# Moving the transposes of attention weights by one slot in a two-layer hybrid decoder, with one PSUM ring, a held coefficient generator and a gate read from PSUM

## Chip, cores, metric

The kernel runs on one core of a Trainium2 chip. The metric is the device time of one execution in microseconds; the median of three executions is given.

## What is computed

Two layers, each with three token mixers in parallel over 512 tokens of width 1024: retention (A), stick-breaking attention (B) and a complex-diagonal state-space model (C). The change lies in mixer B and in what runs around it. Cut to that, the reference is

```python
def stick_breaking(q, k, v, q_norm, k_norm):          # 8 heads of 64, 512 tokens
    q, k, scale = rmsnorm(q, q_norm), rmsnorm(k, k_norm), SB_HEAD_DIM ** -0.5
    for blk in range(S_ // SB_BLOCK):                 # 4 blocks of 128 queries
        start, end = blk * SB_BLOCK, blk * SB_BLOCK + SB_BLOCK
        z = jnp.einsum('bqhd,bkhd->bhqk', q[:, start:end], k[:, :end]) * scale
        causal = jnp.arange(end)[None, :] < (start + jnp.arange(SB_BLOCK))[:, None]
        log_keep = jnp.where(causal, jax.nn.log_sigmoid(-z), 0.0)
        after = lax.cumsum(log_keep, axis=3, reverse=True) - log_keep
        w = jnp.where(causal, jnp.exp(jax.nn.log_sigmoid(z) + after), 0.0)
        outs.append(jnp.einsum('bhqk,bkhd->bqhd', w, v[:, :end]))
    return jnp.concatenate(outs, axis=1)
...
y_b = stick_breaking(...) * jax.nn.silu(sz)           # the gate
merged = sigmoid(ga) * (y_a @ proj_a) + sigmoid(gb) * (y_b @ proj_b) + sigmoid(gc) * (y_c @ proj_c)
x = x + merged @ w_out
```

## The kernel before

**Main pieces and slots.** All large products (the input projection, the three output projections, w_out) run as float32 split into a high and a low part, three matmuls each (`three`). They are cut into main pieces, most of 24 matmuls into one PSUM tile `mm`; a piece of `pb`, the projection of the gated attention output, has 12. `layer` runs through the list `mains`; one turn of that loop is a slot, and `now[0]` is its number. Everything else is written as generators which `spawn` puts into a slot. What a generator issues before `yield 0` goes to the engines ahead of the slot's main piece, what follows goes behind it, and `yield n` passes to n slots later. So the order on every engine is fixed by this loop when the program is built. Behind the main piece and the generators, `W.fill` splits the next weights, and then `background`, the generator of the state-space coefficients (`Coef`, mostly on GpSimd), is advanced until the shares counted in `load` are used up, unless the slot is in `quiet`.

**An attention pair.** `sb_pair(pr)` does two heads, h = 0 and 1; four pairs start 4 slots apart. With s the first slot of a pair:

- s: the preamble, which splits queries and keys into `qd`, `ql` and `ks` (ScalarE, VectorE, GpSimd).
- s+1 and s+3: scores of the last query block of head 0 and of head 1 into PSUM tile `z3` (3 matmuls); s+2 and s+4: the scores of the other three blocks into `z02` and `z1` (9 matmuls). Behind the main piece `weights_of` makes weights from them: two sigmoids on ScalarE, then on VectorE a reverse scan (`kp`, line 1083) and a product into `w3`, `w02` or `w1`.
- `turn(h)`: 10 transposes on TensorE (line 1100) of the weights of head h into three PSUM tiles `wt`; `turned(h)` copies them to SBUF (ScalarE two, VectorE one, line 1107). `turn(0)` stands in s+3 behind the z3 scores of head 1; `turn(1)` in s+5, where the next pair's z3 scores of head 0 (its own s+1) stand ahead of it.
- s+6: 16 matmuls with the values `sv` into PSUM tile `sbo`, behind the next pair's z02 and z1 scores; VectorE copies it to SBUF (line 1143). s+7: VectorE multiplies it by the gate `zb` (a silu made at slots 12 to 17 of the layer). s+8 (last pair: s+7): the result is split for `pb`.

Slots of a layer, by what the main piece is: 0 to 11 queries, keys and values of attention; 12 to 23 gates; 24 to 27 `cu` (the input of mixer C); 28 to 30 `cz`; from 31 on `pb`. The pairs start at slots 11, 15, 19 and 23.

**PSUM.** The eight banks are two rings: `ps_mm` has 3 for main pieces, `ps_sm` has 5 for everything else. A tile takes the bank of the allocation 3, or 5, earlier in its ring, so its first matmul waits until that one has been read.

**Coefficients.** `Coef.emit` makes four quarters. Per quarter it makes `ab` and `ct` (products on GpSimd), transposes them, makes `ca` and `b`, and multiplies these on TensorE (`pk`); the blocks are copied into `mt` (GpSimd). `quiet` holds slots 10 to 13 and 23 to 28 of the layer.

```python
        quiet = {*range(first - 1, first + 3), *range(turn, turn + 6)}
        for name, m in mains:
            ...
            for gen in due.pop(i, []):
                advance(gen, late)
            m()
            while late:
                advance(late.pop(0), late)
            W.fill()
            while i not in quiet and load["G"] < G_SHARE * load["T"] and load["V"] < V_SHARE * load["T"]:
```

Of the kernel before, what the change touches and what calls it, by code (L numbers as in the profile page):

```python
# [10 lines left out]
F32 = mybir.dt.float32  # L11
# [3 lines left out]
ALU = mybir.AluOpType  # L15
PSUM = bass.MemoryType.PSUM

P = 128
# [17 lines left out]
K = dict(  # L36

    nw=12, w=4, raw=4, b=48,

    sb0=0, sb_gap=4, ssm0=6, ssm_gap=3, ret0=9, ret_gap=3, x0=-3, x1=2, ret_pre=4, lead=15,  # L40

    g=0.9, v=0.7,

    n1=1, n2=1, q1=1, q2=1, k1=1, k2=2, s1=1, s2=1, s3=1, s4=2, s5=1, s6=1, s7=2, b1=1, b2=1, b3=1,
# [142 lines left out]
def trunk(ctx: ExitStack, tc, x_in, w_in, par_in, bc_in, ng_in, cst_in, rope_in, out):  # L187
    nc = tc.nc
# [12 lines left out]
    TT = counted(nc.vector.tensor_tensor, "V", 1.04e-3)  # L201
# [8 lines left out]
    bp = ctx.enter_context(tc.tile_pool(name="bp", bufs=B_BUFS))  # L210
    sp = ctx.enter_context(tc.tile_pool(name="sp", bufs=8))
    dp = ctx.enter_context(tc.tile_pool(name="dp", bufs=1, space=bass.MemoryType.DRAM))
    ps_mm = ctx.enter_context(tc.tile_pool(name="ps_mm", bufs=3, space=PSUM))
    ps_sm = ctx.enter_context(tc.tile_pool(name="ps_sm", bufs=5, space=PSUM))

    def bt(name, dt=F32, shape=(P, 512)):
        return bp.tile(list(shape), dt, tag="b", name=name)
# [2 lines left out]
        return sp.tile([P, n], F32, tag="s", name=name, padded_shape=[P, 64])  # L220

    def pmm():
        return ps_mm.tile([P, 512], F32, tag="mm", name="mm")

    def psm(name):
        return ps_sm.tile([P, 512], F32, tag="sm", name=name)


    cst = const.tile([P, NCST], F32, name="cst")
# [11 lines left out]
    def C(n):  # L241
# [9 lines left out]
        out=negm, in_=negm, pattern=[[1, P]], base=0, channel_multiplier=-1, compare_op=ALU.is_ge, fill=0.0  # L251
# [6 lines left out]
    now = [0]  # L258
# [38 lines left out]
    class Weights:  # L297
        def __init__(self):
            self.loaded = self.made = self.taken = self.free = 0
            self.raw, self.units = [], []  # L300
# [384 lines left out]
    class Coef:  # L685


        def __init__(self, l):
            self.l = l
            self.q = [None] * 4  # L690
            self.gen = self.emit()
            self.ready = -1
            self.used = 0
            self.start = 0

        def step(self):
            next(self.gen, None)
# [25 lines left out]
        def quarter(self, q, bb, cc):  # L723
# [14 lines left out]
            def v48(ap):  # L738
                return ap.rearrange("p (g j m) -> p g j m", g=4, j=8)

            while self.used < q - 1 or now[0] < self.start + K["ssm_gap"] * q:
                yield

            ab = [bt("ab0"), bt("ab1")]
# [35 lines left out]
            for i in range(2):  # L780
                h = slice(64 * i, 64 * i + 64)
# [12 lines left out]
            for i in range(2):  # L794
                h = slice(64 * i, 64 * i + 64)
# [45 lines left out]
    def layer(l, last, base):  # L841
# [3 lines left out]
        coef = coefs[l]  # L845
# [153 lines left out]
        zc, zb = [None] * 4, [None] * 4  # L999
# [47 lines left out]
        sbo = [None] * 4  # L1047

        def sb_pair(pr):
# [18 lines left out]
            def scores(ps, off, h, b):  # L1068
                n = 128 * (b + 1)
                c = slice(b * P, b * P + P)  # L1070
                MM(ps[:, off : off + n], qd[h][:, c], ks[h][:, 0:n], start=True, stop=False)
                MM(ps[:, off : off + n], ql[h][:, c], ks[h][:, 0:n], start=False, stop=False)
                MM(ps[:, off + n - P : off + n], identb, negm, start=False, stop=True)
# [19 lines left out]
            def turn(h):  # L1093
                pts = []
                for blocks in (
                    [(b, 0) for b in range(4)], [(1, 1), (2, 1), (3, 1), (3, 3)], [(2, 2), (3, 2)],
                ):
                    pt = psm("wt")
                    for i, (b, kb) in enumerate(blocks):
                        nc.tensor.transpose(pt[:, i * P : i * P + P], wblk(h, b, kb), ident)  # L1100
                    pts.append(pt)
                return pts

            def turned(h, pts):
                wt0[h], wt13[h] = bt("wt0"), bt("wt13")
                ACT(wt0[h], pts[0], AF.Copy)
                nc.vector.tensor_copy(out=wt13[h], in_=pts[1])
                ACT(wt2[:, 256 * h : 256 * h + 256], pts[2][:, 0:256], AF.Copy)

            for h in range(2):  # L1110
                ps = psm("z3")
                scores(ps, 0, h, 3)
                if h == 1:
                    pts = turn(0)
                yield 0
                w3[h] = bt("w3")
                weights_of(ps, [(0, 512)], w3[h])
                if h == 1:
                    turned(0, pts)
                yield K["b2"]  # L1120
                ps, ps1 = psm("z02"), psm("z1")
                scores(ps, 0, h, 0)
                scores(ps, 128, h, 2)
                scores(ps1, 0, h, 1)
                yield 0
                w02[h] = bt("w02")
                weights_of(ps, [(0, 128), (128, 384)], w02[h])
                weights_of(ps1, [(0, 256)], w1[:, 256 * h : 256 * h + 256])
                yield K["b3"]
            pts = turn(1)  # L1130
            yield 0
            turned(1, pts)
# [1 line left out]
            po = psm("sbo")  # L1134
# [5 lines left out]
                    MM(po[half[h], 128 * kb : 512], sv[kb][:, c], w, start=kb == 0, stop=kb == 3)  # L1140
            yield 0
            sbo[pr] = bt("sbo")
            nc.vector.tensor_copy(out=sbo[pr], in_=po)
            yield K["b5"]
            while zb[pr] is None:
                yield 1
            TT(out=sbo[pr], in0=sbo[pr], in1=zb[pr], op=ALU.mult)
            if pr < 3:
                yield 1
            yb[pr] = split(sbo[pr], "yb")  # L1150


# [220 lines left out]

        first = at["sv"] + 3 + K["sb0"]
        turn = first + 3 * K["sb_gap"]
        quiet = {*range(first - 1, first + 3), *range(turn, turn + 6)}
        for name, m in mains:
            i = now[0]
            quarters()
# [51 lines left out]
```

## Time and profile before

| | us |
|---|---|
| median of 3 executions | 1289.89 |
| lowest, highest | 1289.74, 1291.02 |
| profiled execution | 1291.43 |
| span of its records | 1289.7 |
| TensorE busy | 1271.6 |

The profiled execution took 1.73 us more than the span of its records, and 1.54 us more than the median. Its mean granted TensorE clock is 0.996 of full speed, which is 2.4 GHz. Durations below are from this execution. In rows, a line such as L197 is often that of a helper which records every matmul or tensor operation, so groups are told apart by their tiles, written output<-inputs. A matmul's row gives its start and the time until its modelled end; neighbours overlap, so the time of a group is best read from its start to the start of the next.

### The profile page before, as it was taken

The numbers are of one execution on the slowest core, as the hardware profiler recorded it, in microseconds if no ns is written. First come the engines' busy times: TensorE is split into PE (matmuls) and PEld (weight loads), VectorE is DVE, ScalarE is ACT, GpSimd is POOL, SyncE is SP. The second block draws the span as 40 slices with busy tenths as digits, with TensorE's granted clock in tenths as the row PEclk, the third lists the DMA queues.
The fourth block names the chain that finished last, engine by engine and source line by source line (L and its number), as shares of the span: only waits on it lengthen the run. The fifth ranks groups of instructions, "written<-read, shape, count | busy, mean of one in ns | idle before, by whom it ended". The sixth has DMA issues, their size and how long they took to land.

```text
span 1289.7 us, 16710 instructions
## 1 busy us (share of the span) xinstructions
PE 1271.6 (99%) x6388; PEld 1051.8 (82%) x6388; DVE 845.1 (66%) x1192; ACT 536.9 (42%) x919; POOL 388.4 (30%) x453
## 2 busy tenths in 40 slices
PE   8999999999999999999999989999999999999998
PEld 6887788888888888888888877888888888888887
DVE  6988976866784448555374678778657834675542
ACT  5444454454444433332343545534534544433311
POOL 3314743546531012000052136444565311210000
PEclk9999999999999999999999989999999999999999
DMA  5323222124223322234442312122231232222342
GB/s 211 101 96 98 67 66 82 66 82 131 66 66 99 98 75 72 84 97 155 147 166 72 98 49 66 49 83 82 96 101 66 70 127 82 66 82 83 97 137 75
DMA packets 37235, 119.53 MB, mean 93 GB/s; under 512 B 4130, under 2 KB 4770, under 8 KB 37156
## 3 DMA queue, kind: packets, MB, share of 16 engines
q1 hardware_dynamic: 29376, 104.87, 25.1%
q10 hardware_dynamic: 7780, 13.60, 3.1%
q8 instruction: 50, 0.82, 0.3%
q14 instruction: 29, 0.24, 0.1%
HBM read 114.26 MB, written 4.19 MB: 92 GB/s over the span
## 4 chain that ended last, share of the span: by engine, by line
PE 82%; DVE 3%; ACT 1%; issue 0%; DVEq 0%; ACTq 0%
PE mm L197 71%; PE T L411 2%; PE ro L197 2%; PE py L197 1%; DVE kp L1083 1%; PE S L197 1%; PE sbo L197 1%; PE wt L1100 1%; DVE w L197 1%; PE z L197 1%; PE rkv L197 1%; PE rs L197 1%; PE yaT L1269 1%; DVE ks L197 0%; DVE ybl L197 0%; PE pk L197 0%
## 5 line engine op out<-in xcount | busy, mean ns | idle before, releaser
L197 DVE TENSOR_TENSOR wl<-raw,wh 128x1024 fp32r<-128x1024 f32 x196 | 249.6, 1280 | 100.8 <-ACT wh L320 97.1
L197 PE MATMUL mm<-hh,wh 128*128 128x512 f32 x640 | 256.2, 400 | 0.0
L197 PE MATMUL mm<-hh,wl 128*128 128x512 f32 x640 | 250.8, 392 | 0.0
L197 PE MATMUL mm<-hl,wh 128*128 128x512 f32 x640 | 250.8, 392 | 0.0
L320 ACT ACTIVATE wh<-raw 128x1024 fp32r<-128x1024 f32 x196 | 206.3, 1058 | 61.8 <-PE mm L197 24.7
L197 PE MATMUL mm<-wh,hh 128*128 128x512 f32 x512 | 206.7, 404 | 0.4 <-ACT hh L434 0.4
L197 PE MATMUL mm<-wl,hh 128*128 128x512 f32 x512 | 201.8, 394 | 0.3 <-DVE wl L197 0.3
L197 PE MATMUL mm<-wh,hl 128*128 128x512 f32 x512 | 201.7, 394 | 0.0
L197 PEld LDWEIGHTS mm<-hh,wh 128*128 128x128 f32 x640 | 121.2, 189 | 25.6 <-issue 1.8
L197 PEld LDWEIGHTS mm<-hh,wl 128*128 128x128 f32 x640 | 120.7, 189 | 26.1
L197 PEld LDWEIGHTS mm<-hl,wh 128*128 128x128 f32 x640 | 121.0, 189 | 23.5
L197 PEld LDWEIGHTS mm<-wl,hh 128*128 128x128 f32 x512 | 104.8, 205 | 18.6 <-DVE wl L197 2.0
L197 PEld LDWEIGHTS mm<-wh,hl 128*128 128x128 f32 x512 | 104.5, 204 | 18.2 <-DVE hl L197 0.3
L197 PEld LDWEIGHTS mm<-wh,hh 128*128 128x128 f32 x512 | 104.6, 204 | 17.9 <-ACT hh L434 0.8
L1026 ACT ACTIVATE gate<-mm 128x512 f32<-128x512 f32 x48 | 28.6, 596 | 118.2 <-PE mm L197 118.2
L1083 DVE TENSOR_TENSOR_SCAN kp<-kp,zero 128x511 f32<-128x511 f32 (+1 forms) x64 | 60.3, 962 | 22.8 <-ACT kp L1079 22.7
L197 POOL TENSOR_SCALAR ms<-ss 128x8 f32<-128x8 f32 (+3 forms) x56 | 19.1, 341 | 181.9 <-DVE ss L855 101.0
L197 POOL TENSOR_TENSOR rs<-ms,mhalf 128x8 f32<-128x8 f32 (+3 forms) x56 | 64.7, 1155 | 4.7
L853 ACT ACTIVATE sq<-mm 128x512 f32<-128x512 f32 x32 | 19.0, 592 | 85.8 <-PE mm L197 85.7
L197 PE MATMUL mm<-wl,mgh 128*128 128x512 f32 (+1 forms) x136 | 51.5, 378 | 0.2
L197 PE MATMUL mm<-wh,mgh 128*128 128x512 f32 (+1 forms) x136 | 51.3, 377 | 0.0
L197 PE MATMUL mm<-wh,mgl 128*128 128x512 f32 (+1 forms) x136 | 51.3, 377 | 0.0
(258 smaller groups left out, 2244.5 us busy)
## 6 DMA issues: line engine op xcount, KB each, us to landing
raw<-in_w SPq DMA_DIRECT2D x196, 512.0 KB, 3.6
x<-in_x SPq DMA_DIRECT2D x8, 256.0 KB, 7.1
rope<-in_rope ACTq DMA_DIRECT2D x8, 256.0 KB, 4.1
xh<-in_x ACTq DMA_DIRECT2D x8, 256.0 KB, 4.8
x<-xh ACTq DMA_DIRECT2D x8, 256.0 KB, 2.0
xh<-x ACTq DMA_DIRECT2D x8, 256.0 KB, 4.5
out<-xh ACTq DMA_DIRECT2D x7, 256.0 KB, 2.0
br<-in_bc ACTq DMA_DIRECT2D x2, 256.0 KB, 2.9
```

Of the source, the lines that this page charges most:

```text
L197: return f(*a, **k)
L320: ACT(wh, raw, AF.Copy)
L411: nc.tensor.transpose(pt[:, i * P : i * P + P], src[:, i * P : i * P + P], ident)
L853: ACT(s2, ps, AF.Square)
L1026: ACT(sg, ps, AF.Sigmoid)
L1083: nc.vector.tensor_tensor_scan(v, v, zero1.to_broadcast([P, n - 1]), 1.0, ALU.mult, ALU.add)
L1100: nc.tensor.transpose(pt[:, i * P : i * P + P], wblk(h, b, kb), ident)
L1269: nc.tensor.transpose(pt[:, t * P : t * P + P], ytok[t][m // 4][:, (m % 4) * P : (m % 4) * P + P], ident)
```

## The change

It makes four edits.

1. In `sb_pair`, `turn(0)` moves from s+3 (behind the z3 scores of head 1) to s+4 (behind the z02 and z1 scores of head 1), and its copies go behind the weights of that slot. `yield K["b3"] + h` puts `turn(1)` from s+5 to s+6, which is the next pair's s+2; there it stands ahead of that pair's z02 and z1 scores. The `sbo` matmuls move from s+6 to s+7, ahead of the next pair's z3 scores of head 1.
2. The `sbo` copy to SBUF goes; the gate product takes `po` from PSUM, behind the main piece of s+7. The test for `zb` goes with it. The split is at s+8, for the last pair at s+7.
3. The PSUM rings of 3 and 5 become one ring of 8, in which every tile takes the bank of the eighth allocation before it.
4. `quiet` loses slots 23 to 28; instead every quarter of the coefficients but the first is held until slot `coef.hold` = turn + 5, which is 28.

```diff
--- before.py
+++ after.py
@@ -210,8 +210,7 @@
     bp = ctx.enter_context(tc.tile_pool(name="bp", bufs=B_BUFS))
     sp = ctx.enter_context(tc.tile_pool(name="sp", bufs=8))
     dp = ctx.enter_context(tc.tile_pool(name="dp", bufs=1, space=bass.MemoryType.DRAM))
-    ps_mm = ctx.enter_context(tc.tile_pool(name="ps_mm", bufs=3, space=PSUM))
-    ps_sm = ctx.enter_context(tc.tile_pool(name="ps_sm", bufs=5, space=PSUM))
+    ps = ctx.enter_context(tc.tile_pool(name="ps", bufs=8, space=PSUM))
 
     def bt(name, dt=F32, shape=(P, 512)):
         return bp.tile(list(shape), dt, tag="b", name=name)
@@ -220,10 +219,10 @@
         return sp.tile([P, n], F32, tag="s", name=name, padded_shape=[P, 64])
 
     def pmm():
-        return ps_mm.tile([P, 512], F32, tag="mm", name="mm")
+        return ps.tile([P, 512], F32, tag="ps", name="mm")
 
     def psm(name):
-        return ps_sm.tile([P, 512], F32, tag="sm", name=name)
+        return ps.tile([P, 512], F32, tag="ps", name=name)
 
 
     cst = const.tile([P, NCST], F32, name="cst")
@@ -691,7 +690,7 @@
             self.gen = self.emit()
             self.ready = -1
             self.used = 0
-            self.start = 0
+            self.start = self.hold = 0
 
         def step(self):
             next(self.gen, None)
@@ -738,7 +737,7 @@
             def v48(ap):
                 return ap.rearrange("p (g j m) -> p g j m", g=4, j=8)
 
-            while self.used < q - 1 or now[0] < self.start + K["ssm_gap"] * q:
+            while self.used < q - 1 or now[0] < (self.hold if q else 0) or now[0] < self.start + K["ssm_gap"] * q:
                 yield
 
             ab = [bt("ab0"), bt("ab1")]
@@ -1110,23 +1109,23 @@
             for h in range(2):
                 ps = psm("z3")
                 scores(ps, 0, h, 3)
-                if h == 1:
-                    pts = turn(0)
                 yield 0
                 w3[h] = bt("w3")
                 weights_of(ps, [(0, 512)], w3[h])
-                if h == 1:
-                    turned(0, pts)
                 yield K["b2"]
                 ps, ps1 = psm("z02"), psm("z1")
                 scores(ps, 0, h, 0)
                 scores(ps, 128, h, 2)
                 scores(ps1, 0, h, 1)
+                if h == 1:
+                    pts = turn(0)
                 yield 0
                 w02[h] = bt("w02")
                 weights_of(ps, [(0, 128), (128, 384)], w02[h])
                 weights_of(ps1, [(0, 256)], w1[:, 256 * h : 256 * h + 256])
-                yield K["b3"]
+                if h == 1:
+                    turned(0, pts)
+                yield K["b3"] + h
             pts = turn(1)
             yield 0
             turned(1, pts)
@@ -1140,13 +1139,9 @@
                     MM(po[half[h], 128 * kb : 512], sv[kb][:, c], w, start=kb == 0, stop=kb == 3)
             yield 0
             sbo[pr] = bt("sbo")
-            nc.vector.tensor_copy(out=sbo[pr], in_=po)
-            yield K["b5"]
-            while zb[pr] is None:
-                yield 1
-            TT(out=sbo[pr], in0=sbo[pr], in1=zb[pr], op=ALU.mult)
+            TT(out=sbo[pr], in0=po, in1=zb[pr], op=ALU.mult)
             if pr < 3:
-                yield 1
+                yield K["b5"]
             yb[pr] = split(sbo[pr], "yb")
 
 
@@ -1373,7 +1368,8 @@
 
         first = at["sv"] + 3 + K["sb0"]
         turn = first + 3 * K["sb_gap"]
-        quiet = {*range(first - 1, first + 3), *range(turn, turn + 6)}
+        quiet = range(first - 1, first + 3)
+        coef.hold = turn + 5
         for name, m in mains:
             i = now[0]
             quarters()
```

**Places.** TensorE, layer 1, around `turn(1)` of pair 0; `z3`, `z02` and `z1` are scores of pair 1, `mm` is a main piece, `sbo` the output of pair 0. Before, then after:

```order
L197 MATMUL z3_1243<-negm_80,identb_79 128x128
L1100 MATMUL wt_1247<-ident_78,w02_1221 128x128
L1100 MATMUL wt_1247<-ident_78,w1_997 128x128
L1100 MATMUL wt_1247<-ident_78,w02_1221 128x128
...
L1100 MATMUL wt_1257<-ident_78,w3_1136 128x128
L197 MATMUL mm_1260<-hh_82,wh_1085 128x512
...
L197 MATMUL z02_1323<-ks0_1169,qd0_1167 128x128
...
L197 MATMUL z1_1324<-negm_80,identb_79 128x128
L197 MATMUL sbo_1334<-wt0_1142,sv_836 64x512
...
L197 MATMUL mm_1343<-hh_82,wh_1147 128x512
```

```order
L197 MATMUL z3_1240<-negm_77,identb_76 128x128
L197 MATMUL mm_1244<-hh_79,wh_1082 128x512
...
L1099 MATMUL wt_1302<-ident_75,w02_1213 128x128
L1099 MATMUL wt_1302<-ident_75,w1_994 128x128
L1099 MATMUL wt_1302<-ident_75,w02_1213 128x128
...
L1099 MATMUL wt_1312<-ident_75,w3_1120 128x128
L197 MATMUL z02_1315<-ks0_1148,qd0_1146 128x128
...
L197 MATMUL z1_1316<-negm_77,identb_76 128x128
L197 MATMUL mm_1326<-hh_79,wh_1126 128x512
...
L197 MATMUL sbo_1379<-wt0_1225,sv_833 64x512
...
L197 MATMUL z3_1388<-ks1_1149,qd1_1147 128x512
```

The transposes stood directly behind the z3 scores and ahead of that slot's main piece; now a main piece of 24 matmuls stands between, and they are ahead of the z02 scores. `sbo` now has another main piece ahead of it.

VectorE, the same place: the copy `wt13` is part of `turned(1)`, `w02` and `w1` are weights of pair 1's head 0, `w3` of its head 1, `wl` is a weight split, `silu` a gate. Before, then after:

```order
L1083 SCALAR_TENSOR_TENSOR kp_1369<-kp_1369,zero1_85 128x383
L197 TENSOR_TENSOR w02_1368<-w02_1368,kp_1369 128x511
L1083 SCALAR_TENSOR_TENSOR kp_1375<-kp_1375,zero1_85 128x255
L197 TENSOR_TENSOR w1_1241<-w1_1241,kp_1375 128x255
L1143 COPY sbo_1380<-sbo_1334 128x512
L197 TENSOR_TENSOR wl_1383<-raw_1089,wh_1382 128x1024
L197 TENSOR_TENSOR sbo_1380<-sbo_1380,silu_1091 128x512
L197 TENSOR_TENSOR silu_1391<-mm_1343,silu_1391 128x512
L1083 SCALAR_TENSOR_TENSOR kp_1438<-kp_1438,zero1_85 128x511
L197 TENSOR_TENSOR w3_1437<-w3_1437,kp_1438 128x511
L1107 COPY wt13_1444<-wt_1402 128x512
```

```order
L1106 COPY wt13_1352<-wt_1307 128x512
L1082 SCALAR_TENSOR_TENSOR kp_1357<-kp_1357,zero1_82 128x127
L1082 SCALAR_TENSOR_TENSOR kp_1357<-kp_1357,zero1_82 128x383
L197 TENSOR_TENSOR w02_1356<-w02_1356,kp_1357 128x511
L1082 SCALAR_TENSOR_TENSOR kp_1363<-kp_1363,zero1_82 128x255
L197 TENSOR_TENSOR w1_1238<-w1_1238,kp_1363 128x255
L197 TENSOR_TENSOR wl_1369<-raw_1086,wh_1368 128x1024
L197 TENSOR_TENSOR silu_1377<-mm_1326,silu_1377 128x512
L197 TENSOR_TENSOR sbo_1418<-sbo_1379,silu_1088 128x512
L1082 SCALAR_TENSOR_TENSOR kp_1421<-kp_1421,zero1_82 128x511
L197 TENSOR_TENSOR w3_1420<-w3_1420,kp_1421 128x511
```

The `sbo` copy between `w1` and the weight split is gone, the product with the gate reads the PSUM tile (`sbo_1379`) a slot later, and `wt13` stands ahead of the scans of `w02` where before it stood behind `w3`.

GpSimd, layer 1: `ql` and `qd` are the preamble of pair 3, `mt` copies belong to quarter 0, `ab` and `ct` are quarter 1 of the coefficients. Before, then after:

```order
L197 TENSOR_TENSOR ab0_1779<-bbr_1311,y_re_213 128x512
L197 TENSOR_TENSOR ct_1781<-bbi_1312,y_im_214 128x512
L197 TENSOR_TENSOR ab0_1779<-ab0_1779,ct_1781 128x512
L197 TENSOR_TENSOR ab1_1780<-bbr_1311,y_re_213 128x512
L1062 MEMSET ql0_1793 64x512
L1065 COPY qd0_1789<-qd0_1789 64x512
...
L832 COPY mt0_1775<-kk_1868 32x256 x2
...
L832 COPY mt0_1775<-kk_1868 32x2x32 x2
L197 TENSOR_TENSOR ct_1785<-bbi_1312,y_im_214 128x512
L197 TENSOR_TENSOR ab1_1780<-ab1_1780,ct_1785 128x512
```

```order
L1061 MEMSET ql0_1762 64x512
L1064 COPY qd0_1758<-qd0_1758 64x512
...
L831 COPY mt0_1752<-kk_1855 32x256 x2
...
L831 COPY mt0_1752<-kk_1855 32x2x32 x2
L197 TENSOR_TENSOR ab0_2178<-bbr_1290,y_re_210 128x512
L197 TENSOR_TENSOR ct_2180<-bbi_1291,y_im_211 128x512
L197 TENSOR_TENSOR ab0_2178<-ab0_2178,ct_2180 128x512
L197 TENSOR_TENSOR ab1_2179<-bbr_1290,y_re_210 128x512
L197 TENSOR_TENSOR ct_2184<-bbi_1291,y_im_211 128x512
L197 TENSOR_TENSOR ab1_2179<-ab1_2179,ct_2184 128x512
```

Four products of quarter 1 (two on `ab0`, one on `ct`, one on `ab1`) stood ahead of the preamble and of the `mt` copies and now stand behind them; the other two of the six follow as before. Farther on, the `pk` matmuls of quarter 1 stand one `pb` piece of 12 matmuls earlier on TensorE, in both layers. Every engine but VectorE, which has the eight copies fewer, issues the same number of instructions of each kind.

## Rows read from the trace of the kernel before

**Rows 1.** The page, busy time by engine: us (share of the span) xinstructions.

```profile
PE 1271.6 (99%) x6388; PEld 1051.8 (82%) x6388; DVE 845.1 (66%) x1192; ACT 536.9 (42%) x919; POOL 388.4 (30%) x453
```

**Rows 2.** Waits of TensorE, whole span: line waited for, us in total, times, longest.

```profile
PE wt L1100 <- DVE w L197: 10.4, 10, 2.1
PE gain L452 <- POOL negm L249: 2.3, 1, 2.3
```

**Rows 3.** Windows: length, busy us (count) by engine, TensorE's granted clock, DMA, GB/s.

```profile
98.06:99.14 1.08, 1.08 (x12) 1.08 (x12) 0.71 (x2) 1.08 (x3) 0.00 (x0) 1.00 0.81 182
99.14:104.70 5.56, 5.56 (x27) 4.60 (x26) 5.35 (x11) 1.98 (x4) 0.00 (x0) 1.00 0.28 85
111.79:114.12 2.33, 1.48 (x12) 1.18 (x12) 2.23 (x4) 1.72 (x4) 0.00 (x0) 1.00 0.62 214
142.97:147.57 4.60, 2.35 (x12) 2.06 (x12) 4.39 (x6) 1.97 (x4) 0.58 (x1) 0.77 0.33 114
147.57:153.72 6.15, 6.15 (x26) 5.08 (x25) 6.05 (x6) 1.33 (x2) 6.07 (x4) 0.90 0.18 54
178.60:180.68 2.08, 1.30 (x12) 1.11 (x12) 1.91 (x5) 2.08 (x4) 0.00 (x0) 1.00 0.68 217
210.21:211.57 1.36, 1.23 (x12) 0.96 (x10) 1.36 (x2) 1.16 (x3) 0.00 (x0) 1.00 0.03 12
746.52:752.33 5.81, 2.36 (x13) 2.07 (x12) 5.60 (x7) 1.95 (x4) 4.82 (x3) 0.77 0.32 90
752.33:759.82 7.49, 7.49 (x26) 5.99 (x25) 3.67 (x4) 1.33 (x2) 0.68 (x2) 0.73 0.23 70
783.06:786.72 3.66, 1.48 (x12) 1.19 (x12) 3.45 (x5) 1.78 (x4) 0.16 (x1) 1.00 0.42 143
817.16:819.72 2.56, 1.52 (x13) 1.20 (x12) 2.38 (x6) 2.56 (x5) 0.00 (x0) 1.00 0.64 202
849.25:850.60 1.35, 1.22 (x11) 0.96 (x10) 1.35 (x2) 1.16 (x3) 0.00 (x0) 1.00 0.01 3
```

**Rows 4.** Timeline, TensorE: start us, us, line, out<-in, count [idle <-releaser].

```profile
98.12 1.26 PE L1100 MATMUL wt<-ident,w 128*128 128x128 f32 x10
...
759.82 0.22 PE L197 MATMUL z<-ks,qd 128*128 128x128 f32 x1
...
761.00 1.40 PE L197 MATMUL sbo<-wt,sv 128*64 128x512 f32 x6
...
856.26 2.38 PE L197 MATMUL sbo<-wt,sv 128*64 128x512 f32 x16
...
876.03 0.65 PE L197 MATMUL pk<-ca,b 128*32 128x128 f32 x16
```

**Rows 5.** Timeline, VectorE, layer 2: scans, products, and the copy of attention's output.

```profile
727.26 1.27 DVE L1083 TENSOR_TENSOR_SCAN kp<-kp,zero 128x127 f32<-128x127 f32 x2
...
744.25 2.85 DVE L1083 TENSOR_TENSOR_SCAN kp<-kp,zero 128x127 f32<-128x127 f32 x2
...
749.41 1.03 DVE L197 TENSOR_TENSOR w<-w,kp 128x255 f32<-128x255 f32 x1
...
751.50 0.68 DVE L197 TENSOR_TENSOR silu<-mm,silu 128x512 f32<-128x512 f32 x1
...
764.54 0.68 DVE L1143 COPY sbo<-sbo 128x512 f32<-128x512 f32 x1
```

**Rows 6.** Timeline, GpSimd, layer 2: coefficient work of quarter 1.

```profile
804.37 1.45 POOL L197 TENSOR_TENSOR ab<-bbr,y_re 128x512 f32<-128x512 f32 x1 [2.55 <-DVE Ti L197]
...
858.17 1.06 POOL L197 TENSOR_TENSOR ct<-ccr,y_re 128x512 f32<-128x512 f32 x1 [9.03 <-PE sbo L197]
...
860.33 2.16 POOL L197 TENSOR_TENSOR ca<-ct,ct 128x512 f32<-128x512 f32 x1
...
867.74 0.92 POOL L796 COPY b<-bbr 64x256 f32<-64x256 f32 x1 [0.62 <-DVE Tr L197]
868.71 0.75 POOL L796 COPY b<-bbi 64x256 f32<-64x256 f32 x1
```

## The prediction

> **What bounds the kernel now.** I began with busy time by engine: TensorE is busy for 1271.6 of 1289.7 us, VectorE for two thirds of that [rows 1]. So the kernel is bound by TensorE, and a change can gain only where TensorE stands still or runs slowly. The next view is the list of TensorE's waits [rows 2]. After the start-up one entry counts: transposes `wt` waiting for VectorE's product `w`, 10.4 us in 10 waits, the longest 2.1. The 2.3 us at `gain` belong to start-up, and the change does not touch them.
>
> Where do these waits stand? Not at `turn(0)`: there the stretch from the last score matmul to the next main piece is 1.08 us at full clock, and the main piece behind it 5.56 (98.06 and 99.14 in [rows 3]). They stand at `turn(1)`, once in each of the eight pairs (four pairs, two layers). The windows give these stretches whole, which is better than the idle time, because it includes the slow start of the transposes after a wait. Over 1.08, and over 1.02 in the last pair, where no scores stand ahead (98.12 in [rows 4] to 99.14 in [rows 3]), they cost [rows 3]:
>
> - layer 1: 2.33 - 1.08 = 1.25; 4.60 - 1.08 = 3.52; 2.08 - 1.08 = 1.00; 1.36 - 1.02 = 0.34; together 6.11.
> - layer 2: 5.81 - 1.08 = 4.73; 3.66 - 1.08 = 2.58; 2.56 - 1.08 = 1.48; 1.35 - 1.02 = 0.33; together 9.12.
>
> The two longest have a second price. In them the granted clock was 0.77, and in the main pieces that follow 0.90 and 0.73, so part of those ran at 1.2 instead of 2.4 GHz. They took 6.15 and 7.49 against 5.56: 0.59 + 1.93 = 2.52 us. The stall of 3.66 us, with less idle time before, left the clock at 1.00. In all 6.11 + 9.12 + 2.52 = **17.75 us** hang on `turn(1)`.
>
> **The transposes.** The weights of s+4 are made beside that slot's main piece, and `turn(1)` wants them one main piece later. Take the worst place, pair 0 of layer 2. VectorE finishes the last product at 749.41 + 1.03 = 750.44 [rows 5]; TensorE wants it at 746.52 + 0.06. After the change a main piece of 5.56 us lies between, so TensorE comes to the transposes at about 752.1, 1.7 us after the weights. Its other stalls are shorter than this one, and their margins larger. So all eight waits go, and the low clock with them: -17.75. `turn(0)` also stands later than its weights by more than before, and never waited.
>
> What is late next? `sbo` needs the copies of `turn(1)`, one slot later as before: same distance. The gate product needs `sbo`, and the split needs the gate; all move one slot, except that the split stands at s+8 as before (last pair s+7). Only the last pair has a near user, `pb`, and it lies two slots off.
>
> The same matmuls in other neighbourhoods can overlap differently at their ends: the ten transposes of 98.12 show 1.26 us busy but the main piece begins 1.02 after them, an overlap of 0.24 [rows 4], [rows 3]. Eight groups that lose or gain this much give 1.9 us either way. I take +1.0, since a main piece now has transposes behind it and scores follow them, two joints of different shapes where one was.
>
> **The gate from PSUM.** Eight copies of 0.68 us go from VectorE [rows 5], 5.4 us beside TensorE's work: nothing by themselves. The product still runs once. That it now reads PSUM costs nothing visible: the product `silu<-mm,silu` of the same shape reads PSUM too and takes 0.68 at 751.50 [rows 5]. It waits for `sbo` at the head of its slot; queued behind it on VectorE are the scans of the next pair's z3 weights, whose scores stand behind `sbo` on TensorE anyway. Price 0.
>
> **The one ring of eight.** A main piece had three slots before its bank was wanted again; in the attention stage 17 allocations fall on 4 slots, so the ring of 8 comes round in 1.9 slots. The tightest place is the main piece of s+4, whose bank the main piece of s+6 takes. In the worst row its reader `silu` is done at 751.50 + 0.68 = 752.2 [rows 5]. The new user stands behind the transposes (752.1, 1.02 us) and the nine score matmuls (759.82 to 761.00, 1.18 us [rows 4]), so it comes at 754.3: 2.1 us to spare. Price 0 with that margin, and see the slower rival.
>
> **The hold.** By the order on GpSimd only four products per layer move, behind the preamble of pair 3 and the `mt` copies. The first of them stood at 804.37 [rows 6]. Nothing on TensorE waits for them there: the next user is far behind. What counts is the other end, where `pk` of quarter 1 comes earlier. GpSimd starts its second part at 858.17, released by the `sbo` matmuls of the last pair, begun at 856.26 [rows 6], [rows 4]; it ends with the `b` copy at 868.71 + 0.75 = 869.46, 13.2 us after the start of `sbo`, of which 0.62 was a wait for VectorE's `Tr` [rows 6] that I take as gone with the later start, and I take off some 0.7 more, an estimate within the 2.4 us of the group, because the buffer wanted is released by an earlier matmul of it: 11.9. TensorE then has 2.4 (`sbo`), 5.56 (a main piece), 0.8 (eight transposes at the 1.02 per ten of [rows 4]) and 2.8 (half a piece) until `pk`: 11.5, where before the distance from `sbo` to `pk` was 876.03 - 856.26 = 19.8 [rows 4]. So TensorE waits about 0.4 per layer, between 0 and 2.0 (all of the two deductions gone, and a little): +0.8, at most 4.0.
>
> **Sum.** -17.75 + 1.0 + 0.8 = -16.0 us. Against the profiled execution, 1291.43 - 16.0 = 1275.4; that execution lay 1.54 above the median, so against the median 1289.89 - 16.0 = **1273.9 us**. With no cost and the joints a gain: 1289.89 - 17.75 - 1.9 = 1270.2. With all costs at their ends: 1289.89 - 17.75 + 1.9 + 4.0 = 1278.0.
>
> **Rivals.**
>
> - *`turn(1)` still waits in the worst place.* Its margin of 1.7 rests on VectorE's times in one execution. The two short scans took 2.85 us at 744.25 where the same two took 1.27 at 727.26 [rows 5]; GpSimd was busy for 4.82 us of the stretch at 746.52 [rows 3]. A VectorE that is 4.7 us later still (as late again as the stall is now) would make TensorE wait 3.0 and keep the slow main piece, 1.93: 1273.9 + 4.9 = 1278.8. Against it: VectorE loses a copy per pair.
> - *TensorE waits for GpSimd at `pk`.* The six products from 858.17 on take 1.06 to 2.16 us each and end 0.62 before 867.74, 8.95 us in all [rows 6]. All at 2.16 would be 13.0, 4.0 more per layer, and each such wait could bring a slow spell of 1.93 as at 752.33 [rows 3]: 1273.9 + 2 x 6.0 = 1285.9; half of it 1280.
> - *VectorE's lateness moves on.* The stalls come from a VectorE with a backlog. If that backlog then holds back the weight splits `wl`, TensorE waits at main pieces instead, for about the 15.2 us of stalls: 1289.1, no change. Against it: in the list of TensorE's waits no main piece waits for `wl` in earnest, though VectorE has the same backlog now [rows 2].
> - *Slower: the merged ring.* If the reader of a main piece's tile is over 2.1 us later than in the worst row, the main piece of s+6 waits, not once but in each pair, and delays everything behind it. Priced as the worst stall of now, 4.73 + 1.93 = 6.7 us in each of eight pairs, that is 53: 1273.9 + 53 = 1327. It turns the change into a loss from 2.0 us per pair on. Against it: with rings of three and five TensorE waited for no bank at all [rows 2].
> - *Low clock without a long wait.* The ring makes TensorE look at eight banks in turn, and small gaps between groups could bring the low clock where no wait of 2 us stands. One spell like that at 752.33, 1.93 us [rows 3], in each of eight pairs is 15.4: 1289.3, no change. Against it: the trace shows such spells only behind the two longest stalls, and 3.66 us of stretch at 783.06 brought none [rows 3]. The Trainium skill ("TensorE: Matmul & The Clock Gate", section "A second HAM failure mode: psum-queue depth-cycling") speaks for it, and so against this change: a kernel that cycles its PSUM queue through the banks in each iteration leaves TensorE idle briefly between groups of matmuls often enough for the clock to swing. By that rule the spells would come; this trace, with its rings of three and five, does not bear it out.
> - *The change does not do what it says*: the hold moves only four products per layer, by the order, so its part is small whichever way it goes; it has no case of its own.
>
> **How the numbers follow.** Forecast 0.76 (1270.2 to 1278.0); `turn(1)` still waits 0.08 (to 1278.8); `pk` waits 0.08 (1278 to 1286); lateness moves on 0.02 and low clock without a wait 0.02 (both about 1289); slower 0.04 (to 1327). The range 1270 to 1280 takes in the forecast, the first rival and half of the second, and leaves about 0.14 out, the forecast's own tail included. A measurement of this kernel can tell 0.2%, 2.6 us, from no change. Faster by more: 0.76 + 0.08 + 0.08 = 0.92; within: 0.04; slower: 0.04.
>
> **What would show it.** Right: in TensorE's waits the line `wt` for `w` is gone or under 1 us; the stretches from scores to main piece around `turn(1)` all have a granted clock of 1.00; main pieces of 5.56 us follow each; VectorE has no `sbo` copy; `pk` waits under 1 us. Wrong: waits at `mm` for a reader of PSUM, at `pk` for GpSimd or at `mm` for `wl`, or a slow clock in a slot without a wait. If the time were above 1280, one of these would have to hold more than 4 us.

## The result and the profile after

The changed kernel takes 1280.19 us (median of four, 1279.84 to 1281.83) beside 1289.82 for the kernel before. The ratio is 0.9917, 95% interval 0.9905 to 0.9929, so it is faster by 0.7 to 1.0%, some 9.2 to 12.3 us. The forecast was 16.0 us. The profiled execution took 1279.84 us, 11.6 less than the profiled one of before.

Busy time by engine, on the page of the changed kernel, beside [rows 1]:

```profile
PE 1265.6 (99%) x6388; PEld 1046.5 (82%) x6388; DVE 840.9 (66%) x1184; ACT 537.1 (42%) x919; POOL 381.2 (30%) x453
```

The kernel is still bound by TensorE. Its waits over the whole span (line waited for, us in total, times, longest), beside [rows 2]:

```profile
PE mm L197 <- DVE wl L197: 5.9, 3, 2.7
PE gain L451 <- POOL negm L248: 2.2, 1, 2.2
PE T L410 <- DVE xn L197: 1.0, 1, 1.0
```

The line of `wt` waiting for `w`, 10.4 us in ten waits, is gone. A line has come that was not there: main pieces wait for VectorE's weight split `wl`. Two of its three waits are of 2.73 us each and stand at the same place of both layers; the third, 0.39 us at 9.96, is start-up. The windows of the changed kernel (length, busy us and count by engine, granted clock, DMA share, GB/s) show first the worst stretch of `turn(1)`, then the two main pieces that wait, beside [rows 3]:

```profile
747.95:748.96 1.01, 1.01 (x12) 1.01 (x10) 1.01 (x2) 0.81 (x2) 0.00 (x0) 1.00 0.00 0
203.15:211.64 8.49, 5.76 (x25) 4.38 (x24) 6.78 (x7) 2.67 (x6) 1.67 (x3) 1.00 0.48 134
834.71:843.21 8.50, 5.77 (x26) 4.38 (x24) 6.78 (x7) 2.67 (x6) 1.67 (x3) 1.00 0.50 134
```

The transposes of `turn(1)` now take 1.01 us from their start to the next group, at full clock; this is the place that took 5.81 us, and the other seven take the same. The two main pieces took 8.49 and 8.50, where 5.56 is usual: 2.93 each.

The main piece is that of slot 28, the first of `cz`. TensorE around its start (start us, us, line, out<-in [idle <-releaser]):

```profile
203.15 0.39 PE L197 MATMUL mm<-hh,wh 128*128 128x512 f32 x1
203.38 0.40 PE L197 MATMUL mm<-hl,wh 128*128 128x512 f32 x1
206.51 0.50 PE L197 MATMUL mm<-hh,wl 128*128 128x512 f32 x1 [2.73 <-DVE wl L197]
```

Its third matmul needs the low part of a fresh weight and finds it 2.73 us late. VectorE in the slot ahead, 27, where the weights of pair 3's second head are made:

```profile
196.89 1.08 DVE L197 TENSOR_TENSOR ybl<-sbo,ybh 128x512 fp32r<-128x512 f32 x1 [4.66 <-ACT ybh L285]
197.89 3.19 DVE L1082 TENSOR_TENSOR_SCAN kp<-kp,zero 128x127 f32<-128x127 f32 x2
201.18 1.31 DVE L197 TENSOR_TENSOR w<-w,kp 128x511 f32<-128x511 f32 x1
202.41 1.78 DVE L1082 TENSOR_TENSOR_SCAN kp<-kp,zero 128x255 f32<-128x255 f32 x1
...
204.64 0.68 DVE L1106 COPY wt<-wt 128x512 f32<-128x512 f32 x1
205.24 4.89 DVE L197 TENSOR_TENSOR wl<-raw,wh 128x1024 fp32r<-128x1024 f32 x4
```

GpSimd in the same stretch:

```profile
197.50 1.62 POOL L197 TENSOR_TENSOR ab<-ab,ct 128x512 f32<-128x512 f32 x1
199.09 1.18 POOL L197 TENSOR_TENSOR ab<-bbr,y_re 128x512 f32<-128x512 f32 x1
...
202.02 1.62 POOL L197 TENSOR_TENSOR ab<-ab,ct 128x512 f32<-128x512 f32 x1
```

These are products of quarter 1 of the coefficients, five of which now run beside this work. And the same work of VectorE in the kernel before:

```profile
204.95 0.69 DVE L197 TENSOR_TENSOR ybl<-sbo,ybh 128x512 fp32r<-128x512 f32 x1 [4.94 <-ACT ybh L286]
205.56 2.14 DVE L1083 TENSOR_TENSOR_SCAN kp<-kp,zero 128x127 f32<-128x127 f32 x2
...
209.26 0.77 DVE L1083 TENSOR_TENSOR_SCAN kp<-kp,zero 128x255 f32<-128x255 f32 x1
...
210.47 1.22 DVE L197 TENSOR_TENSOR wl<-raw,wh 128x1024 fp32r<-128x1024 f32 x1
```

Before, the first of the four splits was ready at 210.47 + 1.22 = 211.7, and the main piece of slot 28 began at 211.57 behind the stalled transposes of 210.21 [rows 3]; its third matmul, the first that reads the split, stood at 212.12. The split came just in time, because the transposes stood in front. Without their 1.36 us that matmul would have come at 210.76 and waited 0.9 us, an estimate from these rows. In the changed kernel nothing stands in front, and VectorE's list has grown by the copy `wt13` (0.68 us), by scans of 3.19 and 1.78 us in place of 2.14 and 0.77, and by a split `ybl` of 1.08 in place of 0.69, some 3 us in all. As it also begins 1.0 us earlier against the main piece of slot 27 (`ybl` at 196.89 and the piece at 197.32, before at 204.95 and 204.34), about 2 us of that are left; with the 0.9 they make the 2.73.

### The profile page after: what moved, and what is told of

It reads as the page before. It is cut to its first block, busy times and chain, and to the rows that moved or that the text cites. A ratio compares the mean times of both kernels' runs of the same rounds, so it can differ in the third digit from the quotient of the medians.

```text
span 1278.1 us, 16657 instructions
## 1 busy us (share of the span) xinstructions
PE 1265.6 (99%) x6388; PEld 1046.5 (82%) x6388; DVE 840.9 (66%) x1184; ACT 537.1 (42%) x919; POOL 381.2 (30%) x453
## 4 chain that ended last, share of the span: by engine, by line
PE 97%; DVE 2%; DMA 0%; ACT 0%; issue 0%; SPq 0%; DVEq 0%; ACTq 0%
PE mm L197 83%; PE T L410 3%; PE z L197 2%; PE ro L197 2%; PE sbo L197 1%; PE wt L1099 1%; PE py L197 1%; PE S L197 1%; DVE kp L1082 1%; PE rkv L197 1%; PE rs L197 1%; PE yaT L1264 1%; DVE wl L197 0%; DMA raw<-in_w 0%; PE pk L197 0%
## 5 line engine op out<-in xcount | busy, mean ns | idle before, releaser
L1082 DVE TENSOR_TENSOR_SCAN kp<-kp,zero 128x511 f32<-128x511 f32 (+1 forms) x64 | 65.4, 1042 | 11.0 <-ACT kp L1078 10.9
```

The costliest lines, as they stand in the source:

```text
L1082: nc.vector.tensor_tensor_scan(v, v, zero1.to_broadcast([P, n - 1]), 1.0, ALU.mult, ALU.add)
```

## The experiments

Each kernel was timed in five rounds beside the kernel before, and the ratios are to that. Times of different runs of the kernel before lie between 1289.8 and 1291.1, so the ratio is the better number.

**1. The late split issued first.** One edit in the changed kernel:

```diff
             m()
+            if i == turn + 4:
+                W.make()
+                W.load()
             while late:
```

> The changed kernel with one line more: in slot 27 of each layer, the last of `cu`, the first of the four weight splits of that slot is issued ahead of the attention weights of pair 3 instead of behind them. Theory (VectorE's queue): in the changed kernel the split is ready at 206.5 and 838.1 us, 2.73 us after the main piece of slot 28 wants it, because 9 us of attention work stand ahead of it. Ahead of them it is done near 201, so both waits go: 1280.2 - 2 x 2.9 = 1274.4 us, and the list of TensorE's waits holds only the start-up. The transposes of pair 3 keep over 2 us of margin. Rival (the split is late because ScalarE or the buffers of the weights are late): the wait stays at 2 us or more, 1279 to 1280.5.

Measured 1274.19 us, ratio 0.9877 (0.9864 to 0.9891). TensorE's waits:

```profile
PE gain L451 <- POOL negm L248: 2.2, 1, 2.2
PE T L410 <- DVE xn L197: 0.9, 1, 0.9
PE mm L197 <- ACT hh L433: 0.6, 1, 0.6
```

Nothing waits after the start-up. On VectorE the split now stands at 200.50, ahead of the scans. The first two scans are as slow as in the changed kernel; the third, which took 1.78 there, takes 0.78 at its later place:

```profile
197.39 1.08 DVE L197 TENSOR_TENSOR ybl<-sbo,ybh 128x512 fp32r<-128x512 f32 x1 [4.66 <-ACT ybh L285]
200.50 1.23 DVE L197 TENSOR_TENSOR wl<-raw,wh 128x1024 fp32r<-128x1024 f32 x1 [2.02 <-ACT wh L319]
201.66 3.19 DVE L1082 TENSOR_TENSOR_SCAN kp<-kp,zero 128x127 f32<-128x127 f32 x2
204.95 0.69 DVE L197 TENSOR_TENSOR w<-w,kp 128x511 f32<-128x511 f32 x1
205.56 0.78 DVE L1082 TENSOR_TENSOR_SCAN kp<-kp,zero 128x255 f32<-128x255 f32 x1
```

So the two waits were a matter of VectorE's order, and they were the difference between forecast and result: the ratio is 0.0040 lower, 5.2 us, where 2 x 2.93 = 5.9 us had to go (the two profiled executions differ by 5.7). This version beats both kernels.

**2. The GpSimd products beside the scans.** The six products of quarter 1 become `nc.gpsimd.memset(o, 0.0)` of the same tiles:

```diff
+                if q == 1:
+                    for o in ab[h], ct, ab[h]:
+                        nc.gpsimd.memset(o, 0.0)
+                        ...
+                    continue
                 GT(out=v48(ab[h]), in0=mat(bb[0], h), in1=power(Y[0], h, True), op=ALU.mult)
```

> The changed kernel with the six GpSimd products of quarter 1 of the coefficients replaced by zeroing of the same tiles, which reads nothing: the coefficients of that quarter are left out. Theory (contention of VectorE's scans with GpSimd's products): the scans of pair 3's second head fall to the 1.27 and 0.68 us that they take elsewhere, the product after them from 1.31 to 0.69, the split is ready near 203.1, before it is wanted at 203.8: no wait, about 1274.4 us. Rival (the scans are long for another reason): scans of 3.2 and 1.8 as in the changed kernel, both waits stay, 1280.

Measured 1274.08 us, ratio 0.9876 (0.9863 to 0.9890); no wait of over 0.4 us is left past the first 13 us. VectorE, and GpSimd beside it:

```profile
197.89 1.26 DVE L1088 TENSOR_TENSOR_SCAN kp<-kp,zero 128x127 f32<-128x127 f32 x2
199.26 0.75 DVE L197 TENSOR_TENSOR w<-w,kp 128x511 f32<-128x511 f32 x1
199.93 0.77 DVE L1088 TENSOR_TENSOR_SCAN kp<-kp,zero 128x255 f32<-128x255 f32 x1
```

```profile
196.73 0.53 POOL L748 MEMSET ct<- 128x512 f32 x1 [3.51 <-PE z L197]
197.20 0.99 POOL L748 MEMSET ab<- 128x512 f32 x2
198.13 0.52 POOL L748 MEMSET ct<- 128x512 f32 x1
198.60 0.52 POOL L748 MEMSET ab<- 128x512 f32 x1
```

The two scans of `w02` lie wholly beside zeroing and take 1.26 us; beside the products they took 3.19. So the lengthening is the GpSimd products' doing, and it is gone where GpSimd only writes. The Trainium skill ("SBUF — State Buffer", section "Who interferes with whom") states that an instruction of VectorE with two SBUF inputs contends with one of GpSimd that reads SBUF and not with one that only writes. This run agrees (1.26 against 3.19).

**3. The hold undone** (edit 4 back to `quiet` as before, edits 1 to 3 kept).

> The changed kernel with the fourth edit undone (quiet slots 23 to 28, no hold). Theory (the hold lets six products on GpSimd run beside the scans of pair 3 and draws the scans out from 2.14 and 0.77 us to 3.19 and 1.78): with four of the six back at their old place the scans are as short as before, the split is ready some 2.1 us earlier, and the two waits of 2.73 shrink to about 0.6: 1280.2 - 4.3 = 1275.9 us. Rival (it is the missing transposes ahead of slot 28 and the copy wt13 in front of the split, whatever GpSimd does): waits of 2.5 and more, 1279.5 to 1280.5.

Measured 1284.56 us, ratio 0.9956 (0.9942 to 0.9969): slower than the changed kernel by 4.4 (5.0 by the ratios), where faster by 4.3 was expected. TensorE's waits:

```profile
PE mm L197 <- DVE wl L197: 6.1, 5, 2.7
```

At slot 28 the theory holds: the wait is 0.44 and 0.46, where 0.6 was expected. But a wait of 2.74 (layer 1) and 2.22 us (layer 2) has come at slot 24, the first of `cu`, for the splits there. From the end of slot 22 on the four products are beside VectorE again. VectorE, then GpSimd:

```profile
165.12 2.08 DVE L197 TENSOR_TENSOR wl<-raw,wh 128x1024 fp32r<-128x1024 f32 x1
167.13 1.77 DVE L197 TENSOR_TENSOR ql<-sqk,qd 64x512 fp32r<-64x512 f32 x1
```

```profile
164.62 1.51 POOL L197 TENSOR_TENSOR ct<-bbi,y_im 128x512 f32<-128x512 f32 x1
166.20 2.15 POOL L197 TENSOR_TENSOR ab<-ab,ct 128x512 f32<-128x512 f32 x1
```

A weight split of 2.08 us, 1.22 elsewhere, and a `ql` of 1.77, 0.69 elsewhere. And in layer 1 the granted clock falls in the rest of that main piece and behind it:

```profile
173.32:183.41 10.09, 7.35 (x27) 6.39 (x26) 9.09 (x14) 2.23 (x4) 4.89 (x5) 0.88 0.31 93
183.41:186.00 2.59, 2.59 (x21) 2.39 (x19) 0.69 (x1) 2.30 (x8) 0.76 (x4) 0.83 0.12 47
```

So GpSimd's products make VectorE late in both places, and the hold moves them from the first piece of `cu` to the first of `cz`, where they cost less. Beside the other three edits it is worth 4 to 5 us. In the kernel before, a part of the lateness at slot 24 was covered as at slot 28. The third of the four splits was ready there at 182.2 (two splits, 2.55 us from 180.92), and the matmul that first reads it stood at 183.94, behind the stretch of 2.08 us of `turn(1)` of pair 2 [rows 3]. Without that stretch it would have waited 0.3 us, an estimate from these rows.

**4. The transposes alone** (edit 1, all else as before).

> The kernel before with the first edit alone (transposes and sbo a slot later; two PSUM rings, the sbo copy and the quiet slots as before). Theory: the transposes were all of the gain, 17.75 us in the profiled execution, some 16 against the median; the merged ring and the gate give nothing. A short wait of 0.6 us for the weight split in slot 28 of each layer remains, since no transposes stand ahead of that slot any more: about 1275.5 us. Rival (a ring of five is too short for the new order, so scores or transposes wait for a bank): waits of scores for a copy of transposes, over 1 us in each of six pairs, 1282 or more.

Measured 1283.38 us, ratio 0.9948 (0.9936 to 0.9961):

```profile
PE pk L197 <- issue: 3.7, 2, 1.9
PE mm L197 <- DVE wl L197: 3.5, 4, 1.7
```

No transposes wait. The waits for the split have moved to slot 24 as in experiment 3 (1.69 + 0.34 and 1.19 + 0.33 us), and `pk` waits 1.86 us in each layer. Neither case was as expected: of the gain of 16 us only 6.7 is left by the ratio, the rest is eaten partly by VectorE, partly by something at `pk`. At slot 28, where 0.6 was expected, no wait is left. With the `sbo` copy kept, the split `ybl` of pair 2's output falls into slot 28 and stands behind the weight splits there (at 212.62). The first weight split begins at 207.54 and is done some 1.3 us later, just ahead of the third matmul at 208.97.

**5. Transposes and one ring** (edits 1 and 3).

> The kernel before with the first and the third edit (transposes a slot later, one ring of eight; the sbo copy and the quiet slots as before). With the first alone `pk` waited 1.86 us in each layer, by the profile for nothing that it shows, in a slot where five other tiles were asked for just before it. Theory (that wait is for a bank of the ring of five, but VectorE is late in the next slots anyway): the wait at `pk` goes, the waits for the weight split at slot 24 grow to some 2.5 us in each layer, total 1283 to 1284.8 us. Rival (the ring is worth what the wait at `pk` cost): 1279.7.

Measured 1286.00 us, ratio 0.9964 (0.9952 to 0.9977). The wait at `pk` is gone, and the other has grown to 3.65 and 3.13 us:

```profile
PE mm L197 <- DVE wl L197: 6.8, 2, 3.6
```

A wait taken away upstream only lets TensorE reach the late split sooner. The time is above both the theory (to 1284.8) and the rival (1279.7). Behind the longer waits the granted clock fell in both layers: it was 0.86 over the main piece at 173.29 and 0.77 between 806 and 819, where it stayed at 1.00 behind the 1.69 and 1.19 us of experiment 4. The intervals of the two experiments overlap, so the ring gains nothing in this order; that it loses is not shown.

**6. The two rings under a kernel that waits nowhere** (experiment 1 with edit 3 undone).

> The changed kernel with the split of slot 27 issued first, as in fill_one, but with the two PSUM rings of three and five. Nothing waits in fill_one, so that any wait here is the ring's. Theory (in slots 22 the `pk` matmuls take the bank of scores that stand ahead of them in the same slot, and wait until ScalarE has read them): `pk` waits 1.86 us in each layer, 1274.2 + 3.8 = 1278.0 us. Rival (the ring of five is enough, the wait of turns_only came from elsewhere): 1274.2.

Measured 1282.03 us, ratio 0.9930 (0.9918 to 0.9943), 6.8 us behind experiment 1 by the ratios. `pk` waits 2.44 us in each layer:

```profile
169.16 0.44 PE L197 MATMUL pk<-ca,b 128*32 128x128 f32 x4 [2.44 <-POOL qd L1065]
```

The releaser named, GpSimd's `qd`, is a wrong track, since `pk` reads nothing of it. In the order of the ring, `pk` takes the bank that the scores z02 of the same slot took five allocations earlier (`z1` and three `wt` stand between), and ScalarE's last read of that tile is this one:

```profile
168.47 0.59 ACT L1080 ACTIVATE w<-z 128x512 f32<-128x512 f32 x1
```

It ends at 169.06, `pk` starts at 169.16. In experiment 4 the same read ended at 168.30 and `pk` started at 168.40. So the wait is for a bank, and a ring of five is too short for the new order. (The slot is 23; the expectation says 22.) In layer 1 the clock fell behind it, to 0.50, which is 1.2 GHz:

```profile
169.16:170.17 1.01, 1.01 (x16) 0.63 (x17) 0.98 (x3) 1.01 (x4) 0.00 (x0) 0.50 0.00 0
170.17:176.78 6.61, 6.61 (x28) 5.39 (x25) 5.66 (x11) 1.14 (x2) 1.70 (x2) 0.83 0.00 0
```

The second stretch took 6.61 us, 1.05 more than 5.56, and the sixteen matmuls of `pk` 1.01 where they take 0.57 in the changed kernel. In layer 2 the same wait of 2.44 us left the clock at 1.00. The longer wait (2 x 2.44) and the slow spell are why the ring costs more here than the 3.8 us that were expected.

**7. The gate's copy kept** (edit 2 undone in the changed kernel).

> The changed kernel with the second edit undone: `sbo` is copied to SBUF in s+7, multiplied by the gate in s+8, and split in s+9 (last pair s+8). Theory (the copy lies beside TensorE's work, and in slots 23 and 27, where VectorE is late, the product takes the place of the split): the two waits of the changed kernel stay within 0.4 us of 2.73 and nothing else waits, 1280.2 within 1. Rival (every us of VectorE counts in this stage): a new wait at slot 24 or waits of 3.4 us and more at slot 28, 1282 or more.

Measured 1279.47 us, ratio 0.9918 (0.9905 to 0.9932), the same as the changed kernel:

```profile
PE mm L197 <- DVE wl L197: 3.5, 5, 1.3
```

The sum is as expected, the places are not: 1.27 at slot 28 in place of 2.73 (1.26 in layer 2), and 0.3 at slot 24, twice in layer 1 and once in layer 2. In layer 1 the main piece of slot 24 takes 7.44 us from first to last matmul where it took 6.00, the one of slot 28 7.19 where it took 8.65. The copy moves lateness from one place to the other.

**8. The ring alone and the hold alone**, each in the kernel before.

> The kernel before with the third edit alone, one PSUM ring of eight. Theory: no bank was waited for, and none will be, 1289.8 us within 1, and the same waits of `wt` for `w`. Rival (main pieces wait for banks that VectorE reads late, or the clock swings): waits of `mm` for `silu` or `gate`, or granted clock under 1.00 in other stretches than behind the two longest stalls; 1293 or more.

Measured 1290.76 us, ratio 1.0003 (0.9994 to 1.0012), no change: `wt` waits for `w` 10.3 us in ten waits, the longest 2.1, as in [rows 2], and nothing waits for a bank. The mean granted clock of the profiled execution is 0.996, as before, so the ring brought no slow spells of its own.

> The kernel before with the fourth edit alone (quiet only in slots 10 to 13, later quarters held). Theory (four GpSimd products are moved from beside slots 22 and 23 to beside slot 27, and VectorE is slow wherever they are): the stall of `turn(1)` of pair 2, 1.00 and 1.48 us in the trace of before, falls under 0.3; that of pair 3 in slot 28 grows from 0.34 by the 2.1 us by which the scans lengthen: -2.2 + 4.2, about 1291.5 us, slower by 0.15%. Rival (the hold is worth nothing before, as the prediction had it): both stalls as before, 1289.8.

Measured 1293.54 us, ratio 1.0029 (1.0017 to 1.0040), slower:

```profile
PE wt L1100 <- DVE w L197: 12.7, 11, 2.1
```

The stall of pair 3 grew to 1.26 us in each layer and 0.55 at the next split came on top, near the size that was expected; that of pair 2 stayed at 0.77, where it was 0.78 and 0.80 as idle time before and under 0.3 was expected. So the stall of pair 2 in the kernel before is not these products' doing.

**9. Splits first in place of the hold** (experiment 3 with the splits of slots 23 and 27 ahead of the attention weights).

> The kernel without the fourth edit (nohold), with the weight split issued ahead of the attention weights in slots 23 and 27. Theory (VectorE has enough time in the whole stage, only its order puts splits behind attention): the waits of 2.74, 2.22 and 0.45 us of nohold go, 1274.5 us, as fast as with the hold. Rival (GpSimd's products make VectorE late whatever its order): a wait of over 1 us at slot 24 or at the transposes stays, 1277 or more.

Measured 1279.88 us, ratio 0.9918 (0.9904 to 0.9931), no better than the changed kernel:

```profile
PE mm L197 <- DVE wl L197: 4.8, 3, 2.5
```

The wait at slot 28 is gone, 2.48 and 1.95 us at slot 24 stay. `cu` takes four splits at once. My edit put the third first; the fourth, which `cu` itself asks for, still stood behind the scans, at 179.55. Whether the order alone could do without the hold is left open.

**10. A split first in the kernel before.**

> The kernel before with the split of slot 27 issued first, without any of the four edits. Theory (there the attention weights are wanted before the split, by `turn(1)` ahead of slot 28, so that the split ahead of them delays the transposes by its own 1.2 us): the stall of pair 3 grows from 0.33 by 1.2 in each layer, 1290.2 + 2.4 = 1292.6 us. Rival (early splits are good by themselves): 1289.5 or less.

Measured 1295.84 us, ratio 1.0044 (1.0030 to 1.0058). The list of waits has `wt` for `w` 14 times, 14.4 us in all; the stall of pair 3 is now two waits, 1.25 and 0.74 us, in each layer. What gains 5 us with the transposes moved loses as much without their move: the same edit is good or bad by which of VectorE's results TensorE wants first.

## Why the prediction was right, and where it was not

- *The bound and the removable time*: right. All waits at `wt` went, in the changed kernel and with edit 1 alone. The worst place has the margin that was worked out, 1.7 us: the last product there ends at 745.10 + 1.03 = 746.13, the transposes start at 747.95, 1.8 us later:

```profile
745.10 1.03 DVE L197 TENSOR_TENSOR w<-w,kp 128x255 f32<-128x255 f32 x1
```

- *The low clock*: the stretches it was read from are at 1.00 now, and the sum of -17.75 us stands: -17.75 + 2 x 2.93 = -11.9 beside the measured -11.6 of the two profiled executions. Against the median it is too large. Experiment 1, where nothing waits, gained 17.3 us between the profiled executions and 15.9 by the ratio. The sum was read in an execution 1.54 us above the median, and the prediction took the whole of it off the median too.
- *Joints*: +1.0 forecast, about +0.3 left in that sum.
- *`pk`*: +0.8 forecast, 0 found. The distance from `sbo` (849.88) to `pk` is 11.6 us, forecast 11.5 (its terms add up to 11.56); GpSimd is done 0.45 us before. It started its second part earlier in `sbo`, as forecast, and was done 11.2 us after the start of `sbo` instead of 11.9:

```profile
861.49 0.65 PE L197 MATMUL pk<-ca,b 128*32 128x128 f32 x16
```

```profile
860.64 0.40 POOL L795 COPY b<-bbi 64x256 f32<-64x256 f32 x1
```

- *One ring, gate from PSUM*: no bank was waited for, and the copy is worth nothing by itself, as forecast. What the prediction didn't see is that the ring of five would no longer have done (experiment 6). It weighed the ring only as a risk. The rival of a low clock without a long wait did not come either: with the ring alone the mean clock was that of before (experiment 8), and in experiment 1 it was 1.00.
- *The hold*: wrong. "Nothing on TensorE waits for them there" looked for a reader of the four products. They act through VectorE, which they slow, and so through the weight split. The prediction used that very contention (2.85 against 1.27) for one rival at pair 0 and did not ask where the moved products would stand in time. Order on GpSimd says little of that: held in the program until slot 28, five of the six ran at 196 to 204 us beside the main piece of slot 27, which begins at 197.32; the trace names VectorE's `w` as the releaser of the first product (192.31) and TensorE's `z` as that of the second (196.36), so tiles that came free set their time. Nor is the hold's part small, as the prediction had it: alone in the kernel before it loses 3.7 us by the ratio (experiment 8), beside the other edits it gains 4 to 5 (experiment 3).
- *What is late next*: the step that failed. It followed the attention's own chain (copies, `sbo`, gate, split of the output) and left out the other work in VectorE's queue. The trace of before had a part of it: the split was ready at 211.7 and the main piece began at 211.57, so with the transposes (1.36 us) gone from in front, the piece would have waited some 0.9 us. Where the wait lands hangs on the other edits. With edit 1 alone it stands at slot 24 (1.69 and 1.19 us) and none at slot 28 (experiment 4). In the changed kernel it stands at slot 28, 2.73 us in each layer; with the hold undone 0.44 of that is left, with the copy kept 1.27. The rival that named it, lateness that moves on to `wl`, had a chance of 0.02, because the list of waits showed no wait for `wl`. But a list of waits shows only the last of two: as long as the transposes were late in front of the same main piece, the lateness of the split could not show.

The measured median is 0.2 us above the upper end of the range; by the ratio, 0.9917 x 1289.89 = 1279.2, it is inside, near that end. The sign was right, and the size 16.0 for about 10.7 by the ratio. That the time came out near the end of the range is luck: the range reached to 1280 for waits at `turn(1)` and `pk`, which did not come, while the lateness at `wl` that did come had been priced at 1289.

## What to carry to other kernels

Before a wait is moved out of the way, look at what else the same engine delivers to the next instruction in line, and at how early that comes: here a stall hid a smaller lateness behind it. Price work on GpSimd by what it does to VectorE's instructions beside it, and find where it stands in time from its buffers and not from its place in the program. Where several results of one engine are wanted, order its queue by when each is wanted; here issuing one split earlier was worth half as much as the whole change.

## What the runs showed of the hardware

A wait of the same length did not always bring the low clock. Behind 2.44 us at `pk` it fell to 0.50 in layer 1 and stayed at 1.00 in layer 2 (experiment 6); behind 2.74 us in experiment 3 it fell, behind the 2.73 us of the changed kernel it did not, in either layer. Nor is it the same in every execution of one kernel: of the five of experiment 3, two took 1283.2 us at a mean granted clock of 0.999 and three 1284.6 to 1285.3 at 0.997. The prediction tied the low clock to the longest stalls; these runs show that the length of one wait does not settle it, and what does is open. The slowing of VectorE beside GpSimd's products came in several instructions: 3.19 against 1.26 us for two scans, 2.08 against 1.22 for a weight split, 1.77 against 0.69 for `ql`. It goes both ways: GpSimd's product of `bbr` and `y_re` took 1.07 us while VectorE stood idle (192.31 in the changed kernel) and 1.51 beside VectorE's `ks` (168.32 in experiment 3).
